# A decoder layer on one core: activations written in portions beside each piece's load, gating groups closer together, one product on GpSimd, v copied sooner

## The chip, the cores and the metric

The kernel runs on one core of one Trainium2 chip. The metric is the device time of one execution in microseconds (us); the time before is the median of three runs.

## The reference

One hybrid decoder layer over 256 tokens of width 1024, in float32. A first half (two attention mixers, merged, with an output projection and a residual) gives `x1`. The second half, on which the change acts, is a retrieval over 16384 single-neuron experts. A token has 8 heads; each takes the top 16 of the scores of each half key and the top 16 of their sums, so that a token uses 128 experts `ic`, with gates `gc` from a softmax:

```python
q = (xt @ w_q).reshape(T, H, 2, PEER_QDIM // 2)      # 8 heads, two half keys
s = jnp.einsum('thcd,cnd->thcn', q, subkeys)         # 128 scores for each half
...
a = jnp.einsum('cd,chkd->chk', xc, u[ic])
act = jax.nn.gelu(a) * gc
out = jnp.einsum('chk,chkd->cd', act, v[ic])
```

## The kernel before

Weights come as pieces of 128x1024 float32 (512 KB), in the order of the list `items`: 74 for the first half and the queries, then the 128 pieces of u, then the last 8 of v. Three helpers keep each piece some steps ahead of its use. `load_to` issues the load on SyncE's queue into one of four `raw` buffers (line 128). `hi_to` rounds it to float32r on ScalarE (line 137). `lo_to` subtracts on VectorE to get the remainder (line 145) into one of three `lo` buffers, and then lets the next load go, as the `raw` buffer is free. `take` hands a piece to TensorE and, ahead of that, issues copies of v from one DRAM tensor into another, `ad`, on the same SyncE queue (line 162), by a count that depends on the piece's number. Each product is three matmuls (`mm3`, lines 171 to 173): high by high, low by high, high by low.

The second half does not gather u. It computes all 128 x 128 activations of a token densely, one piece of u (128 experts) after another: `cols_mm` gives 128 experts x 256 tokens, 24 matmuls. Two pieces share a PSUM bank, and `u_evac` empties the pair: for the tokens that are not yet gated ScalarE writes gelu into the activation tile `A` (line 1083); for tokens that are gated already ScalarE writes gelu into a buffer `w0` (line 1086; two buffers) and VectorE multiplies it into `A`, which holds the gate (line 1088).

Beside the pieces runs the retrieval, in `vector_work`, called once for each piece. First `select` (top-k on VectorE, small matmuls), paced at 1450 ns of VectorE work a piece. Then gating: 64 groups of 4 tokens, `RATE` groups a piece. A group makes one-hots (lines 1033 and 1035, VectorE), multiplies them on TensorE into a 128x128 table of gates for each token (line 1043) and counts the experts used (line 1044), and two steps later `gate_evac` puts the table into `A` (line 1069 VectorE where the activation is there, line 1071 ScalarE where it is not). When all groups are through, `lists` sorts the used experts on VectorE (lines 1154 and 1156), with a permutation of 32 small matmuls on TensorE in its middle (line 1165), and gives the index list `idx["a"]` (lines 1170 and 1171).

The activations must get from `A` into `ad`, beside v, so that one indirect gather fetches for a slot its v row and its activations together. `a_write` (line 1053) appends a write of some experts by some tokens to the list `writes`, and `some_writes` issues from its front. When 128 tokens are gated, the first half of all columns so far is appended; when 256 are, the second half; from 128 tokens on each `u_evac` appends its own two columns. A write that ends at token 256 goes on GpSimd's queue, any other on SyncE's.

After the 128 pieces comes the last product, with v: 8 pieces directly from the input ("d"), then 98 gathered slots ("s"). `fetch` issues the gathers on GpSimd's queue (line 1267); they need the list and all writes, and they land in the memory of `A`. Each step needs the split of its activations (`w_split`, ScalarE line 1274 into `w0`, VectorE line 1275) and of its v rows (lines 1280, 1312); `v_mm` then runs 6 matmuls a token tile (line 1250). `work_ahead` keeps these some steps ahead.

Of the kernel before, what the change touches and what calls it, by code (L numbers as in the profile page):

```python
# [10 lines left out]
F32R = mybir.dt.float32r  # L11
# [4 lines left out]
AF = mybir.ActivationFunctionType  # L16
OP = mybir.AluOpType
# [3 lines left out]
S, D, HD = 256, 1024, 64  # L21
# [28 lines left out]
ND = 8  # L50
NW = NK - ND

S1, CAP0, CAPC = 19, 73, 98
KEY, PAD = 32768.0, NW * 128.0


class Order:
# [41 lines left out]
def tile_hybrid_nsa_dilated_peer(ctx, tc, x, win, wgate, consts, gains, gcols, n1g, n2g, pe, w1, w2, wun, wud, wo, wq, subk,  # L99
                                 cpos, pu, pv, out):  # L100
    nc = tc.nc
# [53 lines left out]
    def take(ahead=3):  # L155

        i = st["use"]
        st["use"] += 1

        while st["copy"] < min(NW, (i - 3) * 0.66):  # L160
            r = st["copy"] * 128
            nc.sync.dma_start(ad[r:r + 128, 0:D], v_col(st["copy"]))
            st["copy"] += 1
        flush()
        hi_to(i + ahead + 1)
        lo_to(i + ahead)
        return parts.pop(i)
# [710 lines left out]
    def Ae(e, n, t0=0, t1=S):  # L878
        return A1[:, e:e + n, t0:t1] if e < 96 else A2[0][:, e - 96:e - 96 + n, t0:t1]
# [168 lines left out]
    writes = []  # L1048

    def a_write(e, n, t0, t1):  # L1050
        def f():
            q = nc.gpsimd if t1 == S else nc.sync
            q.dma_start(ad[e * 128:(e + n) * 128, D + t0:D + t1].rearrange("(e p) t -> p e t", p=128), Ae(e, n, t0, t1))
        writes.append(f)

    def some_writes(n):
        fs, writes[:] = writes[:n], writes[n:]
        for f in fs:
            f()

    def gate_evac(t0, p):

        pt = p.rearrange("p t e -> p e t")
        C = prog["C"]
        for lo_, hi_ in ((0, 96), (96, 128)):
            m = min(max(C, lo_), hi_)
            if m > lo_:
                av = Ae(lo_, m - lo_, t0, t0 + GT)
                nc.vector.scalar_tensor_tensor(av, pt[:, lo_:m, :], 1.0 / GSCALE, av, op0=OP.mult, op1=OP.mult)
            if hi_ > m:  # L1070
                nc.scalar.activation(Ae(m, hi_ - m, t0, t0 + GT), pt[:, m:hi_, :], AF.Copy, scale=1.0 / GSCALE)
        T = prog["T"] = t0 + GT
        if T % 128 == 0:
            n = 4 if T < S else 8
            for z in ((0, min(C, 96)), (96, min(C, NW))):
                for e in range(*z, n):
                    a_write(e, min(n, z[1] - e), T - 128, T)

    def u_evac(e, p):

        T = prog["T"]
        if T < S:
            nc.scalar.activation(Ae(e, 2, T, S), p[:, :, T:], AF.Gelu_apprx_tanh)
        if T:
            tmp = tp_.tile([128, 2, S], F32, name="w0")
            nc.scalar.activation(tmp[:, :, :T], p[:, :, :T], AF.Gelu_apprx_tanh)  # L1086
            av = Ae(e, 2, 0, T)
            nc.vector.tensor_tensor(av, av, tmp[:, :, :T], op=OP.mult)
        prog["C"] = e + 2
        if e < NW and T >= 128:  # L1090
            a_write(e, 2, 0, T - T % 128)
# [32 lines left out]
    idx = {}  # L1124

    def lists():
# [22 lines left out]
        for level in range(2):  # L1149

            for a, b in ((0, 64), (64, NW)) if level == 0 else ((0, NW),):
                kp = k[:, a:b]
                for r in range(a, b, 8):
                    nc.vector.max(s_[:, r:r + 8], kp)
                    if r + 8 < b:
                        nc.vector.match_replace(out=kp, in_to_replace=s_[:, r:r + 8], in_values=kp, imm_value=PAD)  # L1156
                    yield 260 + 3.5 * (b - a)
            yield 2500
            if level == 0:

                p = psTr.tile([128, NW], F32, name="tr")
                d2 = di.rearrange("p a b -> p (a b)")
                for j in range(16):
                    o = (128 - 5 * j) % 128
                    nc.tensor.matmul(p[:, j:NW:16], d2[:, o:o + 128], s_[:, j:NW:16], start=True, stop=True)
                nc.scalar.activation(k, p, AF.Copy)
                yield 2000
# [27 lines left out]
    mk_on = [True]  # L1195

    def vector_work():
        some_writes(1)
        if not state["sel"]:
            state["budget"] += SEL_NS  # L1200
            while state["budget"] > 0:
                try:
                    state["budget"] -= next(sel)
                except StopIteration:
                    state["sel"] = True
                    open_a2()
                    break
        else:
            state["owed"] += RATE
            n = int(state["owed"])  # L1210
            state["owed"] -= n
            if state.get("end") and not q_oh and not q_ps:
                list_work(1900)
            groups_step(n)

    SEL_NS, RATE = 1450, 0.97
    pend = None
    for e in range(NK):
        if e % 2 == 0:
# [11 lines left out]
            pend = (e - 1, p)  # L1231
    while not (state.get("end") and not q_oh and not q_ps):
        groups_step(1)
        some_writes(1)


    u_evac(*pend)
    if state.get("lists") is None:
        list_work(1)
# [28 lines left out]
                                     in_offset=bass.IndirectOffsetOnAxis(ap=idx["a"][:, s_:s_ + 1], axis=0))  # L1268
        return b[:, 0:D], b[:, D:]

    def w_split(a):
        wh = tp_.tile([128, S], F32R, name="w0")
        wl = tp_.tile([128, S], F32R, name="oh2", bufs=3)
        nc.scalar.activation(wh, a, AF.Copy)  # L1274
        nc.vector.tensor_tensor(wl, a, wh, op=OP.subtract)  # L1275
        return wh, wl

    def split_v(raw):
        hi = ring.tile([128, 1024], F32R, name="hi", bufs=4)
        nc.scalar.activation(hi, raw, AF.Copy)  # L1280
        return hi

    got, his, los, wp = {}, {}, {}, {}
    n_got = n_hi = n_lo = n_w = 0

    def gather():

# [10 lines left out]
    def work_ahead(i):  # L1298
        nonlocal n_hi, n_lo, n_w
        while n_w < min(i + 2, len(order)):  # L1300
            wp[n_w] = w_split(a_of(order[n_w]))
            n_w += 1
        while n_hi < min(i + 4, len(order)):
            k = order[n_hi]
            if k[0] == "d":
                load_to(st["use"] + k[1] + 1)
            his[n_hi] = split_v(v_of(n_hi))
            n_hi += 1
        while n_lo < min(i + 3, len(order)):
            k = order[n_lo]  # L1310
            lo = ring.tile([128, 1024], F32R, name="lo")
            nc.vector.tensor_tensor(lo, v_of(n_lo), his[n_lo], op=OP.subtract)  # L1312
            los[n_lo] = lo
            n_lo += 1
            if k[0] == "d":
                raws.pop(st["use"] + k[1])
                load_to(min(st["use"] + k[1] + 1 + RAW, len(items)))
        if "a" in idx:
            state["freed"] = sum(1 for j in range(min(n_w, n_lo)) if order[j][0] == "s")
            gather()  # L1320

# [7 lines left out]
        else:  # L1329
            his[j] = split.pop(st["use"] + j)  # L1330
    n_hi, n_lo = hi_done, lo_done
    some_writes(len(writes))
    xs = []
    for i in range(len(order)):
        while mk_on:
            list_work(1300)
            if order[i + 3][0] == "d" or "a" in idx:
                break
        if "a" in idx:
            gather()  # L1340
        work_ahead(i)
        tiles = (0, 1) if order[i][0] == "d" else slots[order[i][1]][1]
# [142 lines left out]
```

## Time and profile before

| | us |
|---|---|
| median of 3 runs | 994.7 |
| lowest, highest | 991.67, 996.46 |
| the profiled execution's own time | 995.3 |
| its span in the profile | 993.5 |
| TensorE busy in the span | 963.0 |
| VectorE busy | 732.9 |
| ScalarE busy | 501.4 |
| GpSimd busy | 237.9 |

The profile's page gives each engine's busy time and a picture of the span in 40 slices; further views give busy times, granted clock and DMA load of any stretch, what a waiting instruction waited for, the groups of instructions by line, and all of it in order of time. Times count from the start of the span. PE is TensorE, PEld its weight load, DVE VectorE, ACT ScalarE, POOL GpSimd, SP SyncE; an engine's name with a q is its queue. A busy PE can be a slow one: the granted clock stands beside it, 1.00 for 2.4 GHz and 0.50 for 1.2 GHz.

### The profile page before, as it was taken

The numbers are of one execution on the slowest core, as the hardware profiler recorded it, in microseconds if no ns is written. First come the engines' busy times: TensorE is split into PE (matmuls) and PEld (weight loads), VectorE is DVE, ScalarE is ACT, GpSimd is POOL, SyncE is SP. The second block draws the span as 40 slices with busy tenths as digits, with TensorE's granted clock in tenths as the row PEclk, the third lists the DMA queues.
The fourth block names the chain that finished last, engine by engine and source line by source line (L and its number), as shares of the span: only waits on it lengthen the run. The fifth ranks groups of instructions, "written<-read, shape, count | busy, mean of one in ns | idle before, by whom it ended". The sixth has DMA issues, their size and how long they took to land.

```text
span 993.5 us, 18663 instructions
## 1 busy us (share of the span) xinstructions
PE 963.0 (97%) x7163; PEld 892.5 (90%) x7163; DVE 732.9 (74%) x1518; ACT 501.4 (50%) x861; POOL 237.9 (24%) x250
## 2 busy tenths in 40 slices
PE   9999999999999999999999999999986999999997
PEld 9989998998899999999999999999985788888886
DVE  5487566556657998898888888998737557777775
ACT  6366644444454445445544444444324456666673
POOL 4412224000000240130000000000410767767620
PEclk9899999999999999999999999999987999999999
DMA  8658645549788788788787789997993899999941
GB/s 285 233 186 302 214 143 176 177 151 314 270 284 288 260 270 279 239 294 302 251 252 246 234 259 325 305 313 238 265 322 105 338 415 414 325 329 332 324 159 45
DMA packets 83461, 259.91 MB, mean 262 GB/s; under 512 B 9827, under 2 KB 25060, under 8 KB 83366
## 3 DMA queue, kind: packets, MB, share of 16 engines
q1 hardware_dynamic: 66134, 185.12, 56.2%
q0 software_dynamic: 16368, 72.36, 20.2%
q8 instruction: 58, 0.95, 0.4%
q10 hardware_dynamic: 864, 1.18, 0.3%
q14 instruction: 37, 0.30, 0.1%
HBM read 240.80 MB, written 80.75 MB: 324 GB/s over the span
## 4 chain that ended last, share of the span: by engine, by line
PE 82%; DVE 10%; DMA 3%; ACT 2%; issue 2%; POOL 1%; ACTq 0%; POOLq 0%; DVEq 0%
PE acc L1250 22%; PE pj L171 15%; PE pj L173 15%; PE pj L172 15%; DVE lo L145 3%; PE gp L1043 3%; DMA raw<-in_pv_dram 2%; PE pv L589 2%; PE S L545 2%; PE used L1044 1%; PE tr L573 1%; PE tr L906 1%; DVE oh L976 1%; DVE oh L1156 1%; PE acc L173 1%
## 5 line engine op out<-in xcount | busy, mean ns | idle before, releaser
L171 PE MATMUL pj<-T_h,hi 128*128 128x256 f32 x1104 | 320.9, 291 | 1.8 <-ACT w L1086 1.4
L173 PE MATMUL pj<-T_h,lo 128*128 128x256 f32 x1104 | 314.7, 285 | 2.9 <-DVE lo L145 2.8
L172 PE MATMUL pj<-T_l,hi 128*128 128x256 f32 x1104 | 314.0, 284 | 0.0
L137 ACT ACTIVATE hi<-raw 128x1024 fp32r<-128x1024 f32 x205 | 216.4, 1060 | 184.5 <-PE pj L172 51.2
L145 DVE TENSOR_TENSOR lo<-raw,hi 128x1024 fp32r<-128x1024 f32 x204 | 257.3, 1264 | 56.1 <-ACT hi L137 23.0
L173 PEld LDWEIGHTS pj<-T_h,lo 128*128 128x128 f32 x1104 | 213.3, 193 | 4.6 <-DVE lo L145 4.5
L171 PEld LDWEIGHTS pj<-T_h,hi 128*128 128x128 f32 x1104 | 213.4, 193 | 3.4 <-ACT w L1086 1.6
L172 PEld LDWEIGHTS pj<-T_l,hi 128*128 128x128 f32 x1104 | 213.5, 193 | 0.0
L1267 POOL DMA_INDIRECT A<-ad,eT x98 | 129.3, 1320 | 91.5 <-DVE eT L1171 39.9
L1250 PE MATMUL acc<-hi,w 128*128 128x512 f32 x336 | 132.4, 394 | 6.3 <-ACT w L1274 6.3
L1250 PE MATMUL acc<-hi,oh 128*128 128x512 f32 x336 | 131.9, 393 | 4.1 <-DVE oh L1275 4.1
L1250 PE MATMUL acc<-lo,w 128*128 128x512 f32 x336 | 132.0, 393 | 0.0
L1312 DVE TENSOR_TENSOR lo<-A,hi 128x1024 fp32r<-128x1024 f32 x98 | 119.5, 1219 | 0.0
L1280 ACT ACTIVATE hi<-A 128x1024 fp32r<-128x1024 f32 x98 | 102.5, 1046 | 6.9 <-DMA A<-ad,eT 6.9
L171 PE MATMUL pj<-hi,T_h 128*128 128x256 f32 x336 | 97.2, 289 | 0.0
L172 PE MATMUL pj<-lo,T_h 128*128 128x256 f32 x336 | 95.2, 283 | 0.3 <-DVE lo L145 0.3
L173 PE MATMUL pj<-hi,T_l 128*128 128x256 f32 x336 | 95.2, 283 | 0.0
L1275 DVE TENSOR_TENSOR oh<-A,w 128x256 fp32r<-128x256 f32 x106 | 44.9, 424 | 66.8 <-ACT w L1274 66.8
L1274 ACT ACTIVATE w<-A 128x256 fp32r<-128x256 f32 x106 | 44.2, 417 | 84.9 <-PE acc L1250 81.2
L1250 PEld LDWEIGHTS acc<-hi,w 128*128 128x128 f32 x336 | 63.8, 190 | 20.2 <-ACT w L1274 7.0
L1250 PEld LDWEIGHTS acc<-hi,oh 128*128 128x128 f32 x336 | 63.8, 190 | 18.4 <-DVE oh L1275 5.1
L1250 PEld LDWEIGHTS acc<-lo,w 128*128 128x128 f32 x336 | 63.8, 190 | 13.1
(277 smaller groups left out, 1385.8 us busy)
## 6 DMA issues: line engine op xcount, KB each, us to landing
raw<-in_pu_dram SPq DMA_DIRECT2D x128, 512.0 KB, 4.6
ad<-in_pv_dram SPq DMA_DIRECT2D x120, 512.0 KB, 5.7
raw<-in_win_dram SPq DMA_DIRECT2D x44, 512.0 KB, 4.6
ad<-A POOLq DMA_DIRECT2D x14, 512.0 KB, 16.5
ad<-A SPq DMA_DIRECT2D x21, 256.0 KB, 5.6
raw<-in_w_dram SPq DMA_DIRECT2D x8, 512.0 KB, 4.0
raw<-in_wo_dram SPq DMA_DIRECT2D x8, 512.0 KB, 4.8
raw<-in_wq_dram SPq DMA_DIRECT2D x8, 512.0 KB, 5.7
```

What stands on the lines that cost most here:

```text
L137: nc.scalar.activation(split[i], raws[i], AF.Copy)
L145: nc.vector.tensor_tensor(lo, raws.pop(i), split[i], op=OP.subtract)
L171: nc.tensor.matmul(ps, s_[0], m_[0], start=first, stop=False, skip_group_check=True)
L172: nc.tensor.matmul(ps, s_[0], m_[1], start=False, stop=False, skip_group_check=True)
L173: nc.tensor.matmul(ps, s_[1], m_[0], start=False, stop=last, skip_group_check=True)
L1043: nc.tensor.matmul(p[:, j, :], oh[0][:, j, :], oh[1][:, j, i, :], start=(i == 0), stop=(i == 1))
L1250: nc.tensor.matmul(acc[t][d], w[w_][:, ts_], v[v_][:, d * 512:(d + 1) * 512], start=(t, d) not in begun, stop=last and n == 2, skip_group_ ...
L1267: nc.gpsimd.indirect_dma_start(out=b, out_offset=None, in_=ad, in_offset=bass.IndirectOffsetOnAxis(ap=idx["a"][:, s_:s_ + 1], axis=0))
L1274: nc.scalar.activation(wh, a, AF.Copy)
L1275: nc.vector.tensor_tensor(wl, a, wh, op=OP.subtract)
L1280: nc.scalar.activation(hi, raw, AF.Copy)
L1312: nc.vector.tensor_tensor(lo, v_of(n_lo), his[n_lo], op=OP.subtract)
```

## The change

All writes of `A` go on SyncE's queue, and `some_writes` issues them by a budget of 360 KB a call (in `vector_work`, ahead of each step of the last product, and all that is left at the fifth of its steps); a write at token 256 covers 6 columns, not 8. The gathers wait in program order until no write is left. `RATE` goes from 0.97 to 1.15. The product of line 1088 moves from VectorE to GpSimd. Two waits in the lists' cost table go from 2500 to 3500. The copies of v follow a table: 0.94 a piece until item 56, 0.46 until 82, 0.85 until 150, where all 120 are issued; before it was 0.66 throughout, until item 185. The first two `w_split` of the last product are issued ahead of the last `u_evac`.

```diff
@@ -54,6 +54,10 @@
 KEY, PAD = 32768.0, NW * 128.0
 
 
+
+COPIES = np.interp(np.arange(220), [3, 56, 82, 150], [0, 50, 62, NW])
+
+
 class Order:
 
 
@@ -157,7 +161,7 @@
         i = st["use"]
         st["use"] += 1
 
-        while st["copy"] < min(NW, (i - 3) * 0.66):
+        while st["copy"] < min(NW, COPIES[i]):
             r = st["copy"] * 128
             nc.sync.dma_start(ad[r:r + 128, 0:D], v_col(st["copy"]))
             st["copy"] += 1
@@ -1049,14 +1053,18 @@
 
     def a_write(e, n, t0, t1):
         def f():
-            q = nc.gpsimd if t1 == S else nc.sync
-            q.dma_start(ad[e * 128:(e + n) * 128, D + t0:D + t1].rearrange("(e p) t -> p e t", p=128), Ae(e, n, t0, t1))
-        writes.append(f)
-
-    def some_writes(n):
-        fs, writes[:] = writes[:n], writes[n:]
-        for f in fs:
+            nc.sync.dma_start(ad[e * 128:(e + n) * 128, D + t0:D + t1].rearrange("(e p) t -> p e t", p=128), Ae(e, n, t0, t1))
+        writes.append((n * (t1 - t0) // 2, f))
+
+    def some_writes(kb):
+
+        state["kb"] = state.get("kb", 0.0) + kb
+        while writes and state["kb"] > 0:
+            n, f = writes.pop(0)
+            state["kb"] -= n
             f()
+        if not writes:
+            state["kb"] = min(state["kb"], 0.0)
 
     def gate_evac(t0, p):
 
@@ -1071,7 +1079,7 @@
                 nc.scalar.activation(Ae(m, hi_ - m, t0, t0 + GT), pt[:, m:hi_, :], AF.Copy, scale=1.0 / GSCALE)
         T = prog["T"] = t0 + GT
         if T % 128 == 0:
-            n = 4 if T < S else 8
+            n = 4 if T < S else 6
             for z in ((0, min(C, 96)), (96, min(C, NW))):
                 for e in range(*z, n):
                     a_write(e, min(n, z[1] - e), T - 128, T)
@@ -1085,7 +1093,7 @@
             tmp = tp_.tile([128, 2, S], F32, name="w0")
             nc.scalar.activation(tmp[:, :, :T], p[:, :, :T], AF.Gelu_apprx_tanh)
             av = Ae(e, 2, 0, T)
-            nc.vector.tensor_tensor(av, av, tmp[:, :, :T], op=OP.mult)
+            nc.gpsimd.tensor_tensor(av, av, tmp[:, :, :T], op=OP.mult)
         prog["C"] = e + 2
         if e < NW and T >= 128:
             a_write(e, 2, 0, T - T % 128)
@@ -1155,7 +1163,7 @@
                     if r + 8 < b:
                         nc.vector.match_replace(out=kp, in_to_replace=s_[:, r:r + 8], in_values=kp, imm_value=PAD)
                     yield 260 + 3.5 * (b - a)
-            yield 2500
+            yield 3500
             if level == 0:
 
                 p = psTr.tile([128, NW], F32, name="tr")
@@ -1195,7 +1203,7 @@
     mk_on = [True]
 
     def vector_work():
-        some_writes(1)
+        some_writes(WRITE_KB)
         if not state["sel"]:
             state["budget"] += SEL_NS
             while state["budget"] > 0:
@@ -1213,7 +1221,15 @@
                 list_work(1900)
             groups_step(n)
 
-    SEL_NS, RATE = 1450, 0.97
+    def w_split(a):
+        wh = tp_.tile([128, S], F32R, name="w0")
+        wl = tp_.tile([128, S], F32R, name="oh2", bufs=3)
+        nc.scalar.activation(wh, a, AF.Copy)
+        nc.vector.tensor_tensor(wl, a, wh, op=OP.subtract)
+        return wh, wl
+
+    WRITE_KB = 360
+    SEL_NS, RATE = 1450, 1.15
     pend = None
     for e in range(NK):
         if e % 2 == 0:
@@ -1231,9 +1247,10 @@
             pend = (e - 1, p)
     while not (state.get("end") and not q_oh and not q_ps):
         groups_step(1)
-        some_writes(1)
-
-
+        some_writes(WRITE_KB)
+
+
+    wp = {n: w_split(Ae(NW + n, 1)[:, 0, :]) for n in range(2)}
     u_evac(*pend)
     if state.get("lists") is None:
         list_work(1)
@@ -1268,20 +1285,14 @@
                                      in_offset=bass.IndirectOffsetOnAxis(ap=idx["a"][:, s_:s_ + 1], axis=0))
         return b[:, 0:D], b[:, D:]
 
-    def w_split(a):
-        wh = tp_.tile([128, S], F32R, name="w0")
-        wl = tp_.tile([128, S], F32R, name="oh2", bufs=3)
-        nc.scalar.activation(wh, a, AF.Copy)
-        nc.vector.tensor_tensor(wl, a, wh, op=OP.subtract)
-        return wh, wl
-
     def split_v(raw):
         hi = ring.tile([128, 1024], F32R, name="hi", bufs=4)
         nc.scalar.activation(hi, raw, AF.Copy)
         return hi
 
-    got, his, los, wp = {}, {}, {}, {}
-    n_got = n_hi = n_lo = n_w = 0
+    got, his, los = {}, {}, {}
+    n_hi = n_lo = 0
+    n_w = len(wp)
 
     def gather():
 
@@ -1315,7 +1326,7 @@
             if k[0] == "d":
                 raws.pop(st["use"] + k[1])
                 load_to(min(st["use"] + k[1] + 1 + RAW, len(items)))
-        if "a" in idx:
+        if "a" in idx and not writes:
             state["freed"] = sum(1 for j in range(min(n_w, n_lo)) if order[j][0] == "s")
             gather()
 
@@ -1329,14 +1340,14 @@
         else:
             his[j] = split.pop(st["use"] + j)
     n_hi, n_lo = hi_done, lo_done
-    some_writes(len(writes))
     xs = []
     for i in range(len(order)):
+        some_writes(WRITE_KB if i + 4 < ND else 1e9)
         while mk_on:
             list_work(1300)
             if order[i + 3][0] == "d" or "a" in idx:
                 break
-        if "a" in idx:
+        if "a" in idx and not writes:
             gather()
         work_ahead(i)
         tiles = (0, 1) if order[i][0] == "d" else slots[order[i][1]][1]
```

## Rows read from the trace of the kernel before

**Rows 1.** The profile's page: the span, and busy time (share of the span) of two engines.
```profile
span 993.5 us, 18663 instructions
...
PE 963.0 (97%) x7163; PEld 892.5 (90%) x7163; DVE 732.9 (74%) x1518; ACT 501.4 (50%) x861; POOL 237.9 (24%) x250
```

**Rows 2.** Stretches: start:end, length, busy us and instructions by engine, PEclk, DMA share, GB/s.
```profile
600.00:650.00 50.00, 50.00 (x504) 49.40 (x503) 45.45 (x81) 23.13 (x50) 0.00 (x0) 1.00 1.00 317
...
740.00:750.00 10.00, 4.19 (x36) 3.98 (x34) 5.51 (x19) 4.44 (x6) 0.00 (x0) 0.85 0.73 276
750.00:760.00 10.00, 5.93 (x13) 4.26 (x14) 7.66 (x27) 1.87 (x4) 0.00 (x0) 0.50 0.35 107
...
850.00:900.00 50.00, 50.00 (x222) 41.43 (x221) 37.53 (x51) 34.07 (x50) 35.11 (x25) 1.00 0.91 329
```

**Rows 3.** Waits, 700 to 800 us: waiting line, released by: us in total, times, longest.
```profile
PE acc L1250 <- ACT w L1274: 6.3, 2, 5.8
...
PE acc L1250 <- DVE oh L1275: 4.1, 1, 4.1
...
PE tr L1165 <- DVE oh L1154: 1.9, 1, 1.9
...
PE pj L171 <- ACT w L1086: 1.4, 1, 1.4
```

**Rows 4.** Groups of TensorE's instructions by line, 718 to 781 us.
```profile
L1250 PE MATMUL acc<-hi,w 128*128 128x512 f32 x33 | 14.4, 438 | 6.3 <-ACT w L1274 6.3
...
L172 PE MATMUL pj<-T_l,hi 128*128 128x256 f32 x44 | 13.4, 304 | 0.0
...
L1165 PE MATMUL tr<-oh,oh 128*128 128x8 f32 (+1 forms) x32 | 4.8, 292 | 1.9 <-DVE oh L1154 1.9
```

**Rows 5.** TensorE in order of time, from 718 us: start, us, line, operation.
```profile
718.06 0.28 PE L171 MATMUL pj<-T_h,hi 128*128 128x256 f32 x1
...
718.42 0.28 PE L171 MATMUL pj<-T_h,hi 128*128 128x256 f32 x1
```

**Rows 6.** GpSimd's queue in order of time, from 690 us.
```profile
703.65 8.21 POOL L1053 DMA_DIRECT2D ad<-A  x9 [4.36 <-ACT A L1071]
...
730.31 0.72 POOL L1053 DMA_DIRECT2D ad<-A  x1 [1.40 <-DMA ad<-A]
770.96 1.07 POOL L1267 DMA_INDIRECT A<-ad,eT  x1 [39.93 <-DVE eT L1171]
```

**Rows 7.** DMA, 703 to 745 us: bytes; one group of issues, KB each, us to landing.
```profile
DMA packets 4766, 13.04 MB, mean 310 GB/s; under 512 B 472, under 2 KB 1752, under 8 KB 4762
...
raw<-in_pu_dram SPq DMA_DIRECT2D x4, 512.0 KB, 14.3
```

**Rows 8.** Groups of TensorE's instructions by line, 600 to 700 us.
```profile
L171 PE MATMUL pj<-T_h,hi 128*128 128x256 f32 x225 | 65.7, 292 | 0.0
```

**Rows 9.** VectorE in order of time, from 560 us.
```profile
564.49 0.48 DVE L1069 SCALAR_TENSOR_TENSOR A<-gp,A 128x312 f32<-128x312 f32 x1
...
566.28 1.22 DVE L145 TENSOR_TENSOR lo<-raw,hi 128x1024 fp32r<-128x1024 f32 x1
```

**Rows 10.** Groups of VectorE's instructions by line, 600 to 700 us.
```profile
L1088 DVE TENSOR_TENSOR A<-A,w 128x296 f32<-128x296 f32 (+13 forms) x14 | 8.1, 575 | 4.0 <-ACT w L1086 4.0
```

**Rows 11.** GpSimd in order of time, from 290 us.
```profile
362.35 1.29 POOL L978 TENSOR_TENSOR oh<-oh,code 128x560 f32<-128x560 f32 x1 [1.88 <-DVE oh L976]
```

**Rows 12.** VectorE in order of time, from 362 us.
```profile
362.77 1.95 DVE L145 TENSOR_TENSOR lo<-raw,hi 128x1024 fp32r<-128x1024 f32 x1
```

**Rows 13.** The page's costliest groups: the split of activations on VectorE.
```profile
L1275 DVE TENSOR_TENSOR oh<-A,w 128x256 fp32r<-128x256 f32 x106 | 44.9, 424 | 66.8 <-ACT w L1274 66.8
```

**Rows 14.** Stretches of the first half and of the selection; columns as in Rows 2.
```profile
70.00:80.00 10.00, 10.00 (x82) 9.20 (x81) 8.65 (x15) 6.11 (x16) 3.89 (x5) 1.00 0.88 301
...
300.00:400.00 100.00, 98.30 (x795) 95.78 (x795) 86.79 (x323) 47.76 (x60) 17.35 (x26) 1.00 0.80 271
```

**Rows 15.** The page's DMA issues: the pieces of u over the whole span.
```profile
raw<-in_pu_dram SPq DMA_DIRECT2D x128, 512.0 KB, 4.6
```

## The prediction, made before the changed kernel was run

> **What bounds the kernel now.** I read the page first. TensorE is busy for 963.0 of 993.5 us [rows 1], so whatever the change does elsewhere counts only through the 30 us in which TensorE is not busy, and through the time in which it is busy at a low clock. The view of stretches says where these are: TensorE is full at clock 1.00 from 600 to 650 us and from 850 to 900 us, but between 740 and 760 us it is busy for half the time, at a clock down to 0.50, that is 1.2 GHz [rows 2]. The waits of this part name four reasons, which sum to 6.3 + 4.1 + 1.9 + 1.4 = 13.7 us [rows 3]: a split that isn't there in time, each time at the end of a chain that begins with a late load.
>
> What the part from 718 to 781 us loses is worked out from its work. It holds 131 matmuls of the u pieces (43, 44 and 44 on lines 171 to 173) [rows 4]; three of them take 0.36 us at full clock [rows 5], so 15.7 us. It holds 3 x 33 of the v product [rows 4], 50.00 / 222 = 0.225 us each [rows 2], so 22.3 us. The 32 small matmuls of the list take 4.8 us [rows 4]. Together 42.8 of 63 us: **20.2 us are lost**, 13.7 of them idle and 6.5 by the low clock after each gap.
>
> The cause is in the queue of GpSimd: from 703.65 to 731 us it issues the writes of the second token half, 17 in all, one behind the other [rows 6]. The code spreads them one to a piece, but nothing on that queue waits for a piece. In 703 to 745 us the DMA engines move 13.04 MB at 310 GB/s, and a piece of u lands 14.3 us after its issue [rows 7], where 4.6 us is the median of the run [rows 15]. TensorE then gets its pieces at the pace of the loads.
>
> **The change, part by part.** *Writes on SyncE's queue in portions, and gating closer.* The two go together. From the code's cost table the selection takes 68.8 us of VectorE's budget at 1.45 us a piece, so gating starts at piece 48. It has 64 groups and 3 steps of pipeline: 67 / 0.97 = 69 pieces before (ends at 117), 67 / 1.15 = 58 after (ends at 106). Then 106 columns x 64 KB and 7 pairs x 256 KB wait to be written: 8576 KB, 24 calls at 360 KB, so 21 pieces and 3 steps of the last product. Beside 21 loads of 0.524 MB that is 19.0 MB in 21 x 2.88 + 4.8 = 65 us, or 291 GB/s. The engines moved 310 GB/s in the burst [rows 7] and 317 in a stretch with loads, copies and writes in which TensorE stayed full [rows 2]. So it fits, with 6% to spare. On SyncE's queue a write stands behind a load that waits for a free `raw` buffer, and so is paced. Loads will land later than 4.6 us. A load is issued when `lo` has freed its buffer and its rounding is due some three pieces (8.6 us) later; `lo` has two pieces more. I take 1 us lost; the bounds are 0 and 5 (a rate of 270 GB/s makes 70 us of the 65).
>
> The earlier writes (first half, from piece 78) meet no copies any more, as these end with item 150, piece 76: 512 + 360 KB in 3.7 us are 241 GB/s, below the 317 that did no harm [rows 2].
>
> *RATE 1.15.* TensorE's work only moves. A piece now takes 100 us / (225 / 8) = 3.56 us [rows 8], of which 2.88 are its matmuls, so a group costs 0.70 us and a piece will take 3.69. VectorE needs 1.22 us for `lo` and 1.79 for a group (564.49 to 566.28) [rows 9]: 1.22 + 1.15 x 1.79 = 3.28 us. Every seventh piece has two groups, 4.80 against 4.28 on TensorE; the 0.5 us are caught up in the pieces behind it, and the three `lo` buffers give 4.5 us.
>
> *The product on GpSimd.* It takes from VectorE 8.1 + 4.0 us in 14 pairs, 0.86 us a pair [rows 10]. On GpSimd a product of 560 elements took 1.29 us [rows 11], so one of 512 about 1.18. It isn't free for VectorE: while that GpSimd instruction ran, `lo` took 1.95 us [rows 12] and not 1.22 [rows 9], as if it had stood until the other was through. So a pair changes VectorE's time by -0.86 to +0.32 us. Over 39 pairs that is at most 12 us on an engine with 0.4 us a piece to spare; behind gating, the list's steps (1.9 us a piece by the code's count) and `lo` fill it in two runs of five pieces. I take 1 us on TensorE; bounds 0 and 13 (the first rival). The Trainium skill, SBUF — State Buffer, section "Who interferes with whom", speaks against this part: a VectorE instruction with two SBUF inputs and a GpSimd instruction that reads SBUF share a port pair that one holds for its whole instruction while the other stands fully. The trace agrees with it in the 0.73 us by which `lo` grew; by the rule each product could stop VectorE for all its length, by the row it stopped one instruction for part of it.
>
> *The lists.* They start 11 pieces earlier and by the same table end by piece 123, in place of during the last product; the gather no longer waits for them (39.93 us until 770.96) [rows 6], but for the last write. The permutation waits 3500 in place of 2500 ns of budget, so its 1.9 us of idle [rows 3] go. Whether that idle or its 32 small matmuls brought the clock down there the rows don't show: of the 6.5 us up to 3 may stay. I take 1.
>
> *The order at the end.* The first two splits now take both `w0` buffers ahead of the last `u_evac`, whose gelu waits until TensorE is done with the first; so the third split can only start when the second step is through, and its two instructions of 0.42 us [rows 13] stand open: +0.85 us. The gathers: the last write is issued at the third step, 2.7 + 1.2 us after u ends; landing and the first gather, 4.6 us each (estimates from [rows 15]), make 13 us, and the first slot is due after 8 steps x 2.7 = 21.6 us less some 2.5 for its splits. Nothing lost; the bound is 4 us, if writes land as slowly as in the burst [rows 7].
>
> *Copies sooner.* At 70 to 80 us the DMA share was 0.88 [rows 14] with 1.66 transfers a piece; 1.94 make 1.03, for the 15 or so pieces of that density. At 300 to 400 us it was 0.80 [rows 14]; 1.85 transfers make 0.89. A load has 4 us to spare, so 0; bounds 0 and 1.5. What it buys is the room for the writes.
>
> **The sum.** -20.2 + 1 + 1 + 1 + 0.85 = -16.3 us. Against the profiled execution's own 995.3 that gives 979.0; the median lies 0.6 lower, so 978.5.
>
> **The rivals.** *VectorE becomes the bound while gating.* If each product stops it for all of 1.18 us, a pair takes 2 x 3.28 + 1.18 = 7.74 us against TensorE's 7.38: 0.36 us x 29 pairs = 10 us, and at this case's ratio of low clock to idle (6.5 to 13.7) 15 in all: 993. It decides from 0.8 us a pair. For it: 45.45 of 50 us of VectorE are busy already [rows 2]. Against it: what the product gives back, and that a stop needs a two-input instruction in that very moment. Chance 0.08.
>
> *One queue moves reads and writes at a lower rate* (the slow side). Loads and writes now stand in one queue, from piece 106 on. From below 291 GB/s each load is late; at 225 the 19.0 MB take 84 us, 19 idle and 9 by the clock: 1005. It is slower than before from below about 247. For it: the burst's 310 GB/s came from two queues, and it delayed loads threefold [rows 7]. Against it: 317 GB/s with all writes on SyncE's queue [rows 2]. Chance 0.06.
>
> *The stall only moves.* The bytes are the same; if the portions do not spread them, since SyncE runs ahead or the budget lags, the pieces wait for 20 us at another place: 994. Against it stands that a load on that queue waits for a buffer. The Trainium skill, DMA: Bandwidth & Descriptors, section "Issuing engines are not separate DMA queues", has this rival's rule: transfers of all issuers run on the same 16 engines, and another issuer saves only issue time. The trace agrees as far as the loads of one queue stood behind the writes of the other. Chance 0.05.
>
> **How the numbers follow.** The forecast has 0.81, and 974 to 988 as its own range: 975.1 less noise where all 20.2 us come back, and some 10 more where the bounds of the small terms meet. The range for 8 in 10 goes on to 991, into the first rival; out stay the other two and the ends. A measurement of this kernel can tell about 0.5%, 5 us, from no change: faster is below 989.7. That holds for nearly all of the forecast: 0.82. Within: most of the first and third rival, 0.11. Slower: the second and a rest, 0.07.
>
> **What would show it.** Right: no gap on TensorE from piece 106 to the gathers, clock 1.00 there but for the permutation; loads of u landing in 5 to 9 us; no writes on GpSimd's queue; the first gather issued some 10 us after the last piece of u. Wrong: ScalarE's rounding waiting for loads and the DMA share at 1.0 behind piece 106 (second, third rival); `lo` at 2 us and more in many pieces and TensorE waiting for it while gating (first).

## The result, and the profile after

Over 18 runs of each kernel the median was 984.89 us after (972.09 to 990.26) against 995.15 before (991.67 to 996.7). The ratio is 0.9869, with a 95% interval of 0.985 to 0.9888: 1.3% faster. It leaves out four runs of after, 987.66 to 990.26 us, as slow ones (over 1.5% above its fastest); without them its median is 981.6. In a second series of five rounds the same kernel took 979.23 us at a ratio of 0.9842 (0.9824 to 0.9859). The profiled execution of the first series took 977.8 us. The forecast was 978.5, in a range from 974 to 991. The times after spread more than those before, and they go with the granted clock: 0.999 at 972 us, 0.987 at 988 to 990.

The page of after, head and busy times, beside [rows 1]:

```profile
span 975.9 us, 18699 instructions
...
PE 955.8 (98%) x7163; PEld 887.0 (91%) x7163; DVE 725.5 (74%) x1471; ACT 501.0 (51%) x866; POOL 264.4 (27%) x272
```

The span is 17.6 us shorter, but TensorE's busy time only 7.2 us; the other 10.4 us are idle time that went. The waits of TensorE in after, 700 to 800 us, beside [rows 3] (what waited, its releaser: us in total, times, longest):

```profile
PE acc L1267 <- issue: 1.6, 1, 1.6
PE acc L1267 <- ACT w L1227: 1.3, 1, 1.3
```

All four waits of before, 13.7 us, are gone, and two small ones have come, both behind 780 us, in the last product. Where they lie, and where the clock falls, the stretches show, beside [rows 2]:

```profile
690.00:700.00 10.00, 10.00 (x62) 10.00 (x61) 2.79 (x8) 2.18 (x4) 1.28 (x1) 0.66 0.95 316
700.00:710.00 10.00, 10.00 (x86) 10.00 (x84) 9.48 (x31) 4.74 (x6) 1.51 (x2) 1.00 0.78 212
740.00:750.00 10.00, 10.00 (x46) 8.29 (x45) 6.07 (x8) 6.82 (x10) 1.48 (x2) 1.00 0.86 284
750.00:760.00 10.00, 10.00 (x46) 8.08 (x45) 4.36 (x7) 3.49 (x6) 7.87 (x7) 1.00 0.87 301
780.00:790.00 10.00, 8.36 (x37) 6.51 (x36) 3.19 (x5) 2.73 (x4) 7.87 (x8) 1.00 1.02 415
790.00:800.00 10.00, 8.71 (x38) 6.80 (x37) 6.16 (x8) 5.36 (x8) 5.71 (x5) 1.00 1.02 415
```

From 740 to 760 us TensorE is now full at clock 1.00, where it was half idle. Two losses stand elsewhere. At 690 to 700 us TensorE is busy throughout, but at a mean clock of 0.66: (1 - 0.66) x 10 = 3.4 us of full-speed work are lost. This is where the 32 small matmuls of the list run, 689.9 to 694.3 us. And at 780 to 800 us, while the DMA engines are full with gathers (415 GB/s), 1.64 + 1.29 = 2.9 us are idle.

The DMA of after in the stretch of [rows 7], 703 to 745 us:

```profile
DMA packets 11194, 12.60 MB, mean 300 GB/s; under 512 B 480, under 2 KB 9440, under 8 KB 11190
...
raw<-in_pv_dram SPq DMA_DIRECT2D x8, 512.0 KB, 5.2
raw<-in_pu_dram SPq DMA_DIRECT2D x6, 512.0 KB, 5.3
ad<-A SPq DMA_DIRECT2D x8, 384.0 KB, 6.0
ad<-A SPq DMA_DIRECT2D x8, 256.0 KB, 5.9
```

About as many bytes at a slightly lower rate (300 against 310 GB/s), and yet a load lands in 5.3 us and not in 14.3. A higher rate of the engines is not what helped.

GpSimd's queue in after, 721 to 753 us, beside [rows 6]:

```profile
740.58 1.29 POOL L1096 TENSOR_TENSOR A<-A,w 128x512 f32<-128x512 f32 x1 [6.17 <-ACT w L1094]
749.81 1.34 POOL L1284 DMA_INDIRECT A<-ad,eT  x1 [7.94 <-DMA A<-x1d]
```

The product takes 1.29 us there, and the first gather goes 21 us sooner than the 770.96 of before.

One difference of the two profiled executions is chance. TensorE's stretch from 30 to 50 us, where of all that was changed only the copies of v already differ, before and after:

```profile
30.00:50.00 20.00, 20.00 (x147) 20.00 (x146) 6.84 (x10) 7.19 (x11) 7.33 (x16) 0.83 0.58 199
```

```profile
30.00:50.00 20.00, 20.00 (x170) 19.72 (x169) 9.76 (x14) 8.93 (x13) 7.42 (x16) 1.00 0.71 262
```

Here before lost 0.17 x 20 = 3.4 us by the clock and after nothing. The copies don't decide it: the clock of this stretch was 0.91 in a second profile of the kernel after (below), and 1.00 in after with the old copies. In before it fell at 37 us, without idle time, in a run of matmuls of 48 and 24 columns; the same run left it at 1.00 in after. So the account of the spans is: 20.2 us of before gone, 3.4 lost again at the permutation, 2.9 among the gathers, 3.4 won by chance at the start: -17.3, against the measured -17.6. The change itself brought some 14 us of it.

### The profile page after: what moved, and what is told of

It is laid out like the page before. It is cut to its first block, busy times and chain, and to the rows that moved or that the text cites. A ratio compares the mean times of both kernels' runs of the same rounds, so it can differ in the third digit from the quotient of the medians.

```text
span 975.9 us, 18699 instructions
## 1 busy us (share of the span) xinstructions
PE 955.8 (98%) x7163; PEld 887.0 (91%) x7163; DVE 725.5 (74%) x1471; ACT 501.0 (51%) x866; POOL 264.4 (27%) x272
## 4 chain that ended last, share of the span: by engine, by line
PE 88%; DVE 8%; issue 2%; ACT 1%; POOL 1%; DMA 0%; ACTq 0%; POOLq 0%
PE acc L1267 24%; PE pj L175 17%; PE pj L177 16%; PE pj L176 16%; PE gp L1047 3%; DVE lo L149 3%; PE pv L593 2%; PE S L549 2%; PE used L1048 1%; PE tr L577 1%; PE tr L910 1%; DVE oh L980 1%; PE acc L177 1%; PE acc L175 1%; PE acc L176 1%
## 5 line engine op out<-in xcount | busy, mean ns | idle before, releaser
L1284 POOL DMA_INDIRECT A<-ad,eT x98 | 131.9, 1346 | 60.3 <-DVE oh L1228 33.1
L1096 POOL TENSOR_TENSOR A<-A,w 128x512 f32<-128x512 f32 (+28 forms) x39 | 39.1, 1003 | 256.2 <-ACT w L1094 256.2
```

What stands on the lines that cost most here:

```text
L1096: nc.gpsimd.tensor_tensor(av, av, tmp[:, :, :T], op=OP.mult)
L1284: nc.gpsimd.indirect_dma_start(out=b, out_offset=None, in_=ad, in_offset=bass.IndirectOffsetOnAxis(ap=idx["a"][:, s_:s_ + 1], axis=0))
```

## The experiments

The question behind them: of RATE, the queue, the portions, the smaller writes, the product and the copies, which ones bring the time, and does the reason given in the prediction (a burst that nothing paces) hold?

**The change repeated, and its writes on GpSimd's queue again.** The first run is the kernel after as it is. The second sends the late writes where they were, the third also moves the product back, so that nothing holds GpSimd's queue:

```diff
-            nc.sync.dma_start(ad[...], Ae(e, n, t0, t1))
+            q = nc.gpsimd if t1 == S else nc.sync
+            q.dma_start(ad[...], Ae(e, n, t0, t1))
...
-            nc.gpsimd.tensor_tensor(av, av, tmp[:, :, :T], op=OP.mult)
+            nc.vector.tensor_tensor(av, av, tmp[:, :, :T], op=OP.mult)
```

> The changed kernel itself, for the spread of its times. Its executions so far lie between 972 and 990 us, with a mean granted clock between 0.999 and 0.987; the one profiled (975.9 us, 0.995) shows two losses: TensorE at half clock from 692 to 699 us, behind the 32 permutation matmuls, and 2.9 us of gaps at 786 to 792 us, in the gathers' first burst. Theory A (the spread is TensorE's clock: whether it falls behind the permutation, and behind gaps in the burst): another execution shows the same two places, each longer, shorter or absent, and nothing else; every 0.001 of mean clock goes with about 1 to 1.5 us. Theory B (the spread is in the loads): an execution of 983 us or more shows ScalarE's rounding waiting for pieces of u, behind piece 106, for 5 us and more.

> The writes that end at token 256 go on GpSimd's queue again; the budget of 360 KB and all else stay. Theory A (what pays is the pace): GpSimd now also multiplies each pair, and that product stands in its queue between the writes, so the queue is held to the pieces; time as the changed kernel, within 4 us. Rival (what pays is the queue itself, one hardware queue in which loads and writes stand in order): loads of u land in 10 us and more behind piece 106, and 8 us or more are lost.

> As the run before, and the product of the pairs on VectorE again, so that nothing on GpSimd's queue waits for a piece. Theory A (pace): the writes go out in one burst behind piece 106, loads land in 14 us as before the change, TensorE waits; the burst lies earlier and the list is ready, so some 10 to 18 us of the gain are lost: 990 to 1000 us. Rival (the earlier end of gating pays, not the pace): within 4 us of the changed kernel.

The first run's own question first. Its profiled execution took 982.87 us (span 981.1), 5.2 us more than the span of after. Its clock:

```profile
30.00:50.00 20.00, 20.00 (x158) 19.87 (x158) 7.85 (x13) 8.67 (x15) 7.91 (x17) 0.91 0.70 247
140.00:160.00 20.00, 20.00 (x132) 18.47 (x132) 13.26 (x32) 6.62 (x17) 8.54 (x7) 0.83 0.52 178
690.00:710.00 20.00, 20.00 (x145) 20.00 (x145) 12.25 (x29) 6.08 (x9) 3.97 (x3) 0.83 0.83 257
```

That is 1.8 + 3.4 + 3.4 = 8.6 us lost, where after lost 3.4, all at the permutation. ScalarE's rounding waited for no piece of u from 660 to 760 us, so theory B falls. Theory A holds in that the spread is the clock, but it missed the places: both new losses lie in the first half, which no part of the change but the copies touches.

The three times, on one chip: the change 979.23 us (0.9842; 0.9824 to 0.9859), with GpSimd's queue 979.3 (0.9855; 0.9841 to 0.9868), with the product back as well 979.86 (0.9866; 0.984 to 0.9892). In the third kernel the burst is there again, 17 writes of 384 KB and five of 256 KB from 671 to 701 us, and the profile shows no wait of TensorE in the u pieces; its 3.2 us of idle are among the gathers. The second came as theory A had it, but the third as its rival. So, undone in this order, neither the queue nor the pace is what pays, and **the prediction's reason falls**.

**Only the product back on VectorE.**

```diff
-            nc.gpsimd.tensor_tensor(av, av, tmp[:, :, :T], op=OP.mult)
+            nc.vector.tensor_tensor(av, av, tmp[:, :, :T], op=OP.mult)
```

> Only the product of the pairs goes back to VectorE; the writes stay on SyncE's queue in portions. Theory A (the product is hidden on either engine): within 2 us of the changed kernel. Rival (a product on GpSimd stops VectorE's two-input instructions, and that costs TensorE time): 3 us or more faster than the changed kernel. Other rival (VectorE has no room for it at 1.15 groups a piece): 3 us or more slower.

987.53 us (0.9934; 0.9914 to 0.9955) on the chip where the change took 979.23. The size is the second rival's, but its reason does not show: in the profiled execution TensorE never waits for VectorE behind 600 us. That execution was one of the faster ones (984.72 us), with a span of 981.2 that hardly differs from the 981.1 of the change's repeat, so most of the loss is not in it. Its stretches among the gathers:

```profile
780.00:790.00 10.00, 6.97 (x31) 5.44 (x29) 2.19 (x3) 1.56 (x3) 7.19 (x8) 0.95 1.02 416
790.00:800.00 10.00, 9.62 (x31) 7.76 (x32) 5.76 (x8) 5.49 (x8) 5.40 (x4) 0.70 1.02 414
```

TensorE is idle for 3.4 us here and then runs at half clock; VectorE is busy for a fifth of the first stretch. After's repeat lost 2.9 us of idle there and none by the clock. Another 1.5 us lie outside the span: in all six runs the time is 3.0 to 3.5 us above the span, in the change's repeat 1.8. The kernel with the burst had the product on VectorE too and took 979.86. So with the product on VectorE, portions on SyncE's queue are some 8 us slower than the burst on GpSimd's; why stays open.

**One part undone, or one part alone.** RATE or the copies back in after; RATE or the 6 columns alone in before:

```diff
-    SEL_NS, RATE = 1450, 1.15
+    SEL_NS, RATE = 1450, 0.97
...
-        while st["copy"] < min(NW, COPIES[i]):
+        while st["copy"] < min(NW, (i - 3) * 0.66):
...
-            n = 4 if T < S else 8
+            n = 4 if T < S else 6
```

> The kernel after with the gating groups as far apart as before (RATE 0.97), all else as after: portions of 360 KB on SyncE's queue, 6-column writes, product on GpSimd, copies sooner. Theory R (the earlier end of gating is what pays, because the bytes of the second token half then have 11 pieces more before the gathers): the writes last 10 pieces longer, the gathers wait, and the time is 987 to 995, with TensorE waiting for late splits or late gathers behind the u pieces. Rival C (the writes' own form, 6 columns in place of 8, is what pays, or the pace): 979 to 982, the same as after.

> The kernel after with the rule of before for the copies of v (they then end near piece 150 of 0.66 an item rather than by the table's kinks). Theory R and theory C both: TensorE full in the parts that the copies move from, so 978 to 981, as after. Rival V (the copies done sooner make the room for the writes): DMA share at 1.0 where gating writes, loads landing later than 6 us, and 983 to 990.

> The kernel before with RATE 1.15 alone. Theory R: gating ends 11 pieces sooner, the burst of writes on GpSimd's queue falls among pieces whose gathers are not near, and most of the gain comes: 978 to 985, first gather near 740 us. Rival C: the burst of 17 writes still makes the loads late, only sooner; TensorE waits for late splits for some 10 us around 680 to 720, and the time is 990 to 995.

> The kernel before with writes of 6 columns in place of 8 for the second token half. Theory R: the burst stays where it was and the loads late by as much: 992 to 996. Rival C: the engines move the burst at 345 to 380 GB/s in place of 310, the loads of u land in 10 us or less, and the time is 980 to 988.

All on one chip: after with RATE 0.97 990.33 us (0.9943; 0.9922 to 0.9964); after with the old copies 983.43 (0.9879; 0.984 to 0.9917); before with RATE 1.15 999.21 (1.001; 0.9978 to 1.0042); before with 6 columns 995.34 (1.0007; 0.9986 to 1.0028). The old copies and the 6 columns make no difference that these runs can tell. RATE is needed, as theory R had it, but alone it brings nothing; its time lies above the ranges of both theories. What TensorE then waits for, from 600 to 900 us, first in after with RATE 0.97, then in before with RATE 1.15:

```profile
PE acc L1267 <- ACT w L1227: 9.8, 1, 9.8
PE acc L1267 <- DVE oh L1228: 0.8, 1, 0.8
```

```profile
PE pj L171 <- ACT w L1086: 8.6, 1, 8.6
PE acc L1250 <- ACT w L1274: 7.9, 1, 7.9
```

Without the closer groups the u pieces run well, but the first gather goes only at 763.0 us, and the last product waits 9.8 us for it. With the closer groups alone the stall in the u pieces is still there (8.6 us), only earlier, and another follows in the last product (7.9 us).

**What makes a burst harmful.** Two kernels with RATE 1.15 now had the burst of writes ahead of the gathers: the change with the burst lost nothing by it in the u pieces, before with RATE 1.15 lost 8.6 us and the clock behind it. The copies differ, so one run gave the harmless one the old copies, and one gave before RATE 1.15 and the new copies:

```diff
-        while st["copy"] < min(NW, COPIES[i]):
+        while st["copy"] < min(NW, (i - 3) * 0.66):
...
-    SEL_NS, RATE = 1450, 0.97
+    SEL_NS, RATE = 1450, 1.15
```

> The kernel of the run e2b_unpaced (burst of 17 writes on GpSimd's queue, product on VectorE, all else as after) with the rule of before for the copies of v; nothing else differs from that run. Theory M (room: the burst does no harm once the copies of v are out of its way; with portions the copies do no harm either): the last copies and the burst meet at 670 to 690 us, loads of u land in 12 us or more, TensorE loses 8 to 15 us in the u pieces, and the time is 986 to 995. Rival N (the copies have nothing to do with it; something else of the change keeps the burst harmless): 979 to 982, as that run, with loads landing in 10 us or less.

> The kernel before with RATE 1.15 and the new rule for the copies of v, and nothing else; against the run b1_rate115 only the copies differ. Theory M: the burst of writes, now without copies beside it, no longer makes the loads late, the 12 us lost between 690 and 720 in that run go, and the time is 980 to 988. Rival N: 994 to 1000, with the same loss behind piece 106.

979.57 us (0.9863; 0.9848 to 0.9879) and 989.05 us (0.9951; 0.9937 to 0.9964): the first is as fast as with the new copies, the second, just above theory M's range, has 7.9 us of waiting left in the u pieces. The copies are not the reason (theory M falls), though they help when RATE stands alone. The DMA of the burst, 676 to 706 us, says more. First the kernel that lost nothing, then the one that waits (queue, kind: packets, MB, share of 16 engines; q0 is GpSimd's queue, q1 SyncE's):

```profile
q0 software_dynamic: 1637, 5.78, 51.1%
q1 hardware_dynamic: 1551, 5.54, 49.7%
...
ad<-A POOLq DMA_DIRECT2D x16, 384.0 KB, 13.9
raw<-in_pu_dram SPq DMA_DIRECT2D x9, 512.0 KB, 9.1
```

```profile
q0 software_dynamic: 1881, 6.76, 74.8%
q1 hardware_dynamic: 1834, 2.81, 26.0%
...
raw<-in_pu_dram SPq DMA_DIRECT2D x7, 512.0 KB, 15.4
...
ad<-A SPq DMA_DIRECT2D x5, 128.0 KB, 19.0
```

In both the two queues move nearly the same number of packets, 1637 to 1551 and 1881 to 1834. What differs is the size of SyncE's: 5.54 MB / 1551 = 3.6 KB, but 2.81 MB / 1834 = 1.5 KB. The small ones are the 128 KB writes, leftovers of the first token half: two columns of 128 tokens, in runs of 512 bytes. If the engines take a packet from each queue by turns, each of these small packets costs a load behind it the time of one of the burst's large ones. Before itself shows the same count, 706 to 738 us:

```profile
q0 software_dynamic: 1964, 7.16, 76.5%
q1 hardware_dynamic: 1794, 2.86, 24.4%
...
ad<-A SPq DMA_DIRECT2D x4, 128.0 KB, 16.0
```

The Trainium skill, DMA: Bandwidth & Descriptors, section "Queues, rings and completion order", says that a DMA engine goes round the queues that have work and takes one packet of each before it turns to the next. The counts agree with it: in these three profiles they come out within 10% of each other, whatever the bytes. That the skill's packet, which can hold several descriptors, is what the profile counts as one is suggested by that and not shown otherwise.

The leftovers are there because before issues one write a piece, while the pieces themselves append new ones. So the last run takes the kernel that waits and lets two writes go to a piece; the burst with its 8 columns stays:

```diff
-        some_writes(1)
+        some_writes(2)
```

> The kernel of the run b3_rate_copies (before with RATE 1.15 and the new rule for the copies) with two writes of activations to a piece in place of one while gating runs; the burst of 8-column writes on GpSimd's queue stays. Theory Q (the two queues are served packet by packet in turn; in before, b1 and b3 SyncE's queue still holds leftover writes of the first token half, in packets of 512 bytes, when the burst of 4096-byte packets begins, and each of those small packets costs a turn, so the loads behind them starve): no 128 KB writes are left on SyncE's queue behind 676 us, in 676 to 706 us SyncE's queue moves 5 MB or more where b3 had 2.81, at about as many packets as GpSimd's; loads land in 11 us or less, the 7.9 us wait of TensorE goes, and the time is 978 to 983. Rival (the large 8-column writes themselves starve the loads): 988 to 991, with the wait and the 2.8 MB as in b3.

984.86 us (0.9884; 0.9847 to 0.992), where one write a piece gave 0.9951, on another chip. The burst, 676 to 706 us:

```profile
q0 software_dynamic: 1976, 7.06, 70.5%
q1 hardware_dynamic: 1021, 3.72, 30.9%
...
raw<-in_pu_dram SPq DMA_DIRECT2D x9, 512.0 KB, 10.0
ad<-A POOLq DMA_DIRECT2D x8, 512.0 KB, 19.5
```

No 128 KB write is left on SyncE's queue, its packets are 3.6 KB again, the loads land in 10.0 us, not 15.4, and the wait of 7.9 us is gone. GpSimd's queue moved even more than in that kernel. So **it is the leftovers that make the loads too late; the burst alone does not**. It still makes them later (10.0 us, where 4.6 is the median of before), but TensorE does not wait. RATE, the copies and the second write a piece together bring before to 0.9884, whose interval overlaps that of the change (0.985 to 0.9888). The expectation missed in the number of packets and the bytes of SyncE's queue, 1021 to 1976 and 3.72 MB, not 5 (it seems to have had no work part of the time), and in the time, above 983. The wait of TensorE behind the burst shows where that went, to the first step of the last product, from 735.3 us, while the gathers, begun at 722.6 us, fill the DMA engines (413 GB/s):

```profile
PE acc L1251 <- issue: 6.4, 1, 6.4
```

ScalarE stood for 6.9 us at the same time, ahead of emptying the last pair of u pieces (740.8 us), and the trace has no releaser for that either.

**Fewer gathers under way.** Every profile of a kernel whose gathers start before 760 us has one to three idle spots on TensorE around the time when they fill the DMA engines. After, with 8 buffers for gathers and not 17:

```diff
-    NV = (96 * S - NT * D) // (D + S)
+    NV = 8
```

> The kernel after with 8 buffers for gathers in place of 17, so that never more than 8 stand in the queue. Theory G (the gaps on TensorE behind 755 us come from the burst of 17 and more gathers that fills the DMA engines): DMA share behind 765 us falls from 1.0 to some 0.75, no gap on TensorE there, 3 to 4 us less than after: 0.978 to 0.983 of before. Rival H (the gaps have another cause, such as the change of program part there): the gaps stay, 0.984 to 0.988 of before. Slower than after, by late gathers, from some place later on: over 0.989.

975.53 us (0.9826; 0.981 to 0.9842), and five runs within 974.92 to 978.65. TensorE waits for nothing from 660 to 900 us, and behind 780 us, 15 us later than expected, the engines are no longer full:

```profile
770.00:780.00 10.00, 10.00 (x46) 8.29 (x45) 5.73 (x7) 4.61 (x8) 6.57 (x5) 1.00 0.98 376
780.00:790.00 10.00, 10.00 (x46) 8.29 (x45) 6.15 (x8) 5.41 (x8) 5.83 (x5) 1.00 0.77 230
790.00:800.00 10.00, 10.00 (x46) 8.29 (x45) 5.36 (x9) 5.15 (x8) 5.93 (x4) 1.00 0.80 247
```

Theory G holds in the profile, and this kernel is the fastest of all that were run: 1.7% below before. By the ratios it is 0.2 to 0.4% below after, which was measured in other series, so how much of that is the buffers is not sharply known. Why many gathers make TensorE wait is not settled. That the engines are full is not enough, as they are until 780 us here too, without a gap. In after the late splits (ScalarE, from 781.9 us) belong to gathers issued 18 to 24 us earlier, where with 8 buffers a gather lands in 6.6 us; but the profile does not name the gathers as what they waited for, and much of the idle time stands under "issue", with no releaser.

## Why the prediction came out right, and where it did not

*The total.* 978.5 was forecast from a sum of -16.3 us; the profiled spans differ by 17.6, of which 3.4 are chance. The median of the first comparison, 984.89, is 6 us above the forecast, that of the second, 979.23, on it. That it came so near is in part luck. The loss that goes was sized rightly, but for another reason than the one given; and the small terms, 3.85 us in the sum, measured 6.3, in other places than forecast (0, 0, 3.4, 0 and 2.9 below).

*The 20.2 us.* The size was right, and so was the chain: late loads, late rounding, late splits, and a clock that falls after each gap. The step that failed is "The cause is in the queue of GpSimd", with its remedy, "and so is paced". A burst of the same form, unpaced, on the same queue, cost nothing. What starved the loads stood in their own queue: small writes that took turns with the burst's large packets. I had read the 310 GB/s as the limit; the row that would have told is the split by queue, 1964 packets and 7.16 MB against 1794 packets and 2.86 MB. So the change took that loss away with a part that I had counted as pacing only: a budget of 360 KB a piece lets more than one of the 128 KB writes go to a piece, and in the change with the burst none is left on SyncE's queue from 676 to 706 us. That clearing them is what helps is shown for before with two writes a piece; inside the change the budget was not undone alone.

*RATE.* Counted as moving work only. Within the change it is worth 7 to 10 us (the ratio is 0.9943 without it, 0.9869 and 0.9842 with it), as without it the last writes and so the gathers come too late. Alone it is worth nothing: the leftovers then meet the burst sooner (from 676 to 706 us six writes of 128 KB stand in SyncE's queue, and loads land in 14.8 us).

*Loads late, +1.* Measured 0: loads land in 5.3 us at 300 GB/s, and TensorE has no wait from 600 to 780 us. One sum behind it is slightly off: 21 loads and 21 portions of 360 KB are 18.8 MB, not 19.0, so 287 GB/s and not 291, which changes nothing.

*VectorE stopped by GpSimd, +1, and the first rival.* Measured 0 on TensorE. Its waits for `lo` are the same in both kernels, 2.0 us in three places from 443 to 454 us, ahead of the first product, and behind that after has none for VectorE. But the stops are there, at another instruction than the forecast looked at. `lo` takes 1.26 us on average from 465 to 690 us and 1.22 before, with a longest of 2.32; the product mostly begins when a `lo` is through or under way, and what it meets is the first one-hot of a group. Before and after, 465 to 665 us:

```profile
L1033 DVE TENSOR_TENSOR oh<-iotah,eT 128x512 f16<-128x512 f16 x55 | 22.9, 417 | 0.0
```

```profile
L1037 DVE TENSOR_TENSOR oh<-iotah,eT 128x512 f16<-128x512 f16 x61 | 33.9, 556 | 0.0
```

That is 61 x 0.139 = 8.5 us of VectorE's time (an estimate), the longest 1.30 us in place of 0.42: it ended 0.27 us behind the product that ran beside it (645.73 to 646.89 us). The rule of the Trainium skill weighed there (SBUF — State Buffer, "Who interferes with whom") agrees with these stops; VectorE, busy for 91% of that stretch, had room for them. The product's place is not free for all that: back on VectorE, alone, it made the change some 8 us slower, for a reason that is open.

*The clock at the permutation, +1.* Measured 3.4, just above its bound of 3, and so this term was sized too small. No idle time stands ahead of it in after, so the idle time that the change took away was not what brought the clock down; just ahead of the fall ran the 32 small matmuls. But it does not always fall: the same 32 in the kernel with the burst and the old copies (from 694.8 us) left the clock at 1.00:

```profile
690.00:700.00 10.00, 10.00 (x88) 10.00 (x87) 5.20 (x7) 3.82 (x5) 4.00 (x5) 1.00 1.03 401
```

Of the fourteen profiled kernels it stayed at 1.00 behind them in four, and fell in the others, from which part of the spread of the times may come. Matmuls spread out in four groups were not tried.

*The order at the end, +0.85.* Measured 0: from 730 to 780 us TensorE has no wait.

*The gathers, 0.* Measured 2.9, from a cause that I had not thought of: not late gathers but many under way at once. With 8 buffers the idle time is gone; by what way many of them make TensorE wait stays open.

*The other rivals.* One queue is no slower than two in the change: 979.23 against 979.3 us. With the product on VectorE it was (987.53 against 979.86), but not by late loads: in that profile they land in 5.5 us (676 to 745 us). Nor did the stall move as a whole; only the 2.9 us are new. The rule of the Trainium skill cited with that rival (DMA: Bandwidth & Descriptors, "Issuing engines are not separate DMA queues"), that another issuer saves issue time and nothing else, holds for the first two times. It does not tell all that the rows show: while both queues are full, which queue a small packet stands in decides how many bytes the loads get.

## What to carry to other kernels

When loads are late beside a burst on another queue, read the DMA by queue, packets beside bytes: if the packets are equal and the bytes are not, small packets in the load's own queue are what to remove, by issuing them sooner, before the burst is paced. Test each part of a bundle both ways, undone in the new kernel and alone in the old: RATE was worth 7 us or more in the one and nothing in the other. And try a prefetch with no more buffers than it needs to stay ahead: with 8 gathers in place of 17 the DMA engines were full for a shorter time and TensorE had no gap.

## What the runs showed that I had not expected

- Two queues with work share the DMA engines by packets: 1881 to 1834 packets, but 6.76 to 2.81 MB.
- The same late writes make packets of a different size on the two queues: on SyncE's queue in after, 9440 of 11194 packets of 703 to 745 us are under 2 KB, 8960 of them not under 512 bytes, while on GpSimd's queue in the change with the burst, where they have 6 columns too, they average 3.5 KB a packet (6.94 MB / 1979, 676 to 706 us).
- While gathers run at 413 to 416 GB/s TensorE has idle spots of up to 6.4 us; the profile names no releaser for much of that.
- TensorE at 100% busy fell to half clock behind 32 matmuls of 7 or 8 columns in some executions and not in others.
- A product on GpSimd lengthened VectorE's one-hot from 0.42 to up to 1.30 us, 8.5 us in all, and TensorE lost nothing by it.
